# A hybrid trunk on one Trainium2 core: layer 0's scan outputs and output projections issued in pieces, with TensorE's order fixed by the program

## The chip, the cores and the metric

The kernel runs on one core of a Trainium2 chip. Its time is the device time of one run in microseconds (us); the number that counts is the median over runs. TensorE (PE) does the matrix products and the transposes, VectorE (DVE), ScalarE (ACT) and GpSimd (POOL) the elementwise work, and SyncE (SP) issues most transfers (DMAs).

## The reference

Two layers of a diffusion trunk over 1024 latent tokens and 128 context tokens, 1024 wide. Layer 0 runs window attention and a bidirectional state-space scan side by side and joins them in one output projection. The change lies in the last third of layer 0: the per-chunk output of the scan, its gated norm, the projection, and the gated residual with the norm that layer 1 starts with.

```python
def ssd_scan(x, dt, a_head, bm, cm, h0):          # once forward, once on flipped tokens
    ...                                            # chunks of 128 tokens; ch, bh: C and B of each head's group
    cum = jnp.cumsum(la, axis=2)
    diff = cum[:, :, :, None, :] - cum[:, :, None, :, :]
    decay = jnp.exp(jnp.where(causal, diff, -jnp.inf))
    scores = jnp.einsum("bclhn,bcshn->bclsh", ch, bh) * decay
    y_diag = jnp.einsum("bclsh,bcshp->bclhp", scores, xd)
    ...                                            # h_in: the state that enters each chunk
    y_off = jnp.einsum("bclhn,bchpn,bclh->bclhp", ch, h_in, jnp.exp(cum))
    y = (y_diag + y_off).reshape(b, L, H, P)

# y = y_forward + flip(y_backward) + d_skip * xs

def ab_output(attn, g, y, z, gnorm_w, w_out):
    a_out = attn.reshape(b, L, A_WIDTH) * jax.nn.silu(g)
    s_out = rms_norm(y.reshape(b, L, SSD_INNER) * jax.nn.silu(z), gnorm_w)
    return jnp.concatenate([a_out, s_out], axis=-1) @ w_out

# then xl = xl + gate * out, and layer 1: rms_norm(xl, norm_w[1]) * (1 + scale) + shift
```

There are 16 heads of 64 columns in two groups, so y of a chunk is 128 tokens by 1024.

## The kernel before, in words

Tokens are cut into nine tiles of 128: eight latent ones (0 to 7, NLT = 8) and the context tile, number 8. A tile is one chunk of the scan. Everything is fp32; a projection is done in three matmuls per weight tile, with each operand split into a high part and a rest (`split`, L244 to L253: the high part by ACT, the rest by a DVE subtraction, L250).

Who sets the order: the kernel is written tile by tile, and a scheduler with a model of the durations then puts the instructions of every engine into an order of its own; only data, buffers and a few marked instructions bind it. An engine runs what it is given strictly in that order. Transfers are issued by SP, likewise in an order, so one that waits for its buffer holds those behind it.

`scan_out` (L965) makes one chunk's scan output:
- It loads B and C (BC), forms both groups' C·B products on PE (Gp, L973), which ACT copies to SBUF (G), and loads xs, the silu of z (zs) and the states (H). POOL starts y with d_skip·xs (L985).
- For each group, and each direction, PE forms a 128x512 product with the state (off, L992), DVE scales it by the decays (L994) and POOL adds it to y (L995).
- For each group and each half of its heads (four heads), a buffer of cumulated decays (cu, two buffers for all) is loaded (L1000). POOL masks it, once per direction (L1003), ACT takes eight exponentials (L1005), DVE adds the two directions and multiplies by G (L1007, L1008), and PE does four small matmuls into yacc (L1011). So a chunk has four yacc groups, and each cu buffer comes free when its yacc group has been done. DVE adds yacc to y and multiplies by zs (L1012, L1013).
- The norm: ACT squares and sums y (L1015), POOL forms the root (`rstd_of`, L391, L392), DVE scales y (L1017), PE transposes y in two halves of four (pt, L1022), and each half is split into sT.

`project_out` (L1078) projects a tile: for each half of the 1024 output columns 12 weight tiles by three matmuls, 36 of 128x512 into acc (L256 to L258), then `residual` (L1056): DVE multiplies by the gate, POOL adds to x (L1061). ACT squares x, POOL forms the root, DVE scales it into xn (L1096), and `norm_T` (L1043) transposes xn in two halves on PE (pt, L1049), applies scale and shift on DVE (L1052, L1053, one buffer, nf) and stores each half as h1 (L1054). `project_operands` (L1070) loads and splits the attention half of the operands (raw, at).

PSUM: each tag has two buffers of 128x512 (L246): "pre" for Gp and off, "o" for yacc, "tr" for every pt, "mm" for acc.

The loop goes over context tile, tiles 0 to 7 and the end; in each step the program writes the scan output of tile c and then the projection of the tile before it. The scan outputs of the context tile and of tile 0 have been made already, beside the gates (`first_outputs`). During the last projection the loop drops its buffers and starts loading layer 1's weights.

## Time and profile before

| | |
|---|---|
| median of 3 runs | 1850.03 us (1843.2 to 1850.26) |
| the profiled execution | 1849.66 us, its span 1847.8 us |
| granted TensorE clock, mean | 0.958 of full speed |
| stage of the change (about 672 to 1000 us) | PE 292.1 us busy of 328, clock 0.92; DVE 230.9; ACT 149.3; POOL 175.3 |
| ahead of it, 672 us | PE 619.1 us busy, clock 0.97 |
| behind it, 848 us | PE 802.7 us busy, clock 0.96 |

The profile shows one execution. A row of a group of instructions reads: line, engine, operation, what it writes <- what it reads, partitions x elements, count | busy us, mean ns of one | idle us of the engine just before them, and what ended most of it. A row of the timeline reads: start us, length us, engine, line, operation, tiles, shape, count, and in brackets a wait ahead of it with what released it. A row of a stretch reads: its bounds, its length, busy us (and count) of PE, PE's weight loads, DVE, ACT, POOL, then the granted clock, the share of the transfers and GB/s. A row of waits reads: who waits <- for whom: us in all, number of waits, the longest. A row of the chain reads: start, us, engine, what. The names arenaF, arenaG, arenaR, arenaS are memory areas; tiles lie in them.

### The profile page before, as it was taken

Reading aid. Unit: us, or ns where it says so; the run is one execution under the profiler, and the core shown is the slowest. Engines: PE = TensorE matmul, PEld = TensorE weight load, DVE = VectorE, ACT = ScalarE, POOL = GpSimd, SP = SyncE. Lnnn points to the kernel's source line nnn. Section 1 sums busy time; section 2 is a strip of 40 time slices with the busy share of each in tenths; the row PEclk is TensorE's granted clock in tenths of the full one; section 3 lists DMA queues with packets and bytes.
Section 4 is the critical chain, followed back from the end, with each engine's and each line's share of the span. In section 5 each row is a group of like instructions: output and inputs, shape, how many; then the busy total and the mean of one; then the engine's idle time right before and its main releaser. Section 6 shows DMA issues by size and latency. Waiting matters only on the chain.

```text
span 1847.8 us, 27078 instructions
## 1 busy us (share of the span) xinstructions
PE 1713.8 (93%) x9031; PEld 1315.1 (71%) x9031; DVE 1045.4 (57%) x1989; ACT 817.2 (44%) x1873; POOL 744.2 (40%) x741
## 2 busy tenths in 40 slices
PE   6899999999998878998899999999999998998898
PEld 3799999877775766666688898655665665654486
DVE  4665545655546467777665434655665664564243
ACT  4532323665655354444444322444545544545321
POOL 3510000133343345665623010466666665565432
PEclk9999999999999888999999999899999998999899
DMA  7423423434435697565463532020120121104342
GB/s 260 125 81 93 121 62 111 131 101 132 115 105 146 195 284 240 166 208 159 167 180 85 165 110 79 11 61 23 52 71 23 45 75 28 37 29 122 109 154 91
DMA packets 210655, 210.26 MB, mean 114 GB/s; under 512 B 36162, under 2 KB 175504, under 8 KB 210516
## 3 DMA queue, kind: packets, MB, share of 16 engines
q1 hardware_dynamic: 210372, 208.40, 37.8%
q8 instruction: 72, 1.18, 0.3%
q14 instruction: 67, 0.55, 0.1%
q0 software_dynamic: 144, 0.13, 0.0%
HBM read 151.94 MB, written 51.72 MB: 110 GB/s over the span
## 4 chain that ended last, share of the span: by engine, by line
PE 65%; DMA 11%; DVE 8%; POOL 4%; ACT 3%; issue 3%; SPq 2%; POOLq 0%; DVEq 0%; ACTq 0%
PE acc L256 12%; PE acc L258 12%; PE acc L257 12%; PE acco L1469 6%; PE sc L1448 3%; PE pp L1427 3%; PE sc L1450 3%; PE sc L1449 3%; DMA arenaG<-cum_d 2%; DVE arenaR L250 2%; DMA arenaF<-rd_d 2%; DMA rd_d<-arenaF 2%; PE st L808 1%; DVE arenaF L209 1%; POOL arenaG L1003 1%
## 5 line engine op out<-in xcount | busy, mean ns | idle before, releaser
L256 PE MATMUL acc<-arenaR 128*128 128x384 f32 (+4 forms) x1248 | 426.7, 343 | 20.0 <-ACT arenaR L249 8.0
L1484 POOL TENSOR_TENSOR arenaG<-arenaG 128x512 f32<-128x512 f32 x256 | 332.6, 1318 | 233.8 <-ACT arenaG L1455 201.1
L257 PE MATMUL acc<-arenaR 128*128 128x384 f32 (+3 forms) x1176 | 398.2, 339 | 0.1
L258 PE MATMUL acc<-arenaR 128*128 128x384 f32 (+4 forms) x1152 | 385.9, 336 | 0.2
L256 PEld LDWEIGHTS acc<-arenaR 128*128 128x128 f32 x1248 | 240.0, 193 | 61.7 <-issue 16.0
L1455 ACT ACTIVATE arenaG<-sc 128x512 f32<-128x512 f32 (+1 forms) x304 | 174.7, 580 | 224.2 <-PE sc L1450 206.7
L209 DVE TENSOR_REDUCE arenaF<-pp 128x1 f32<-128x384 f32 (+1 forms) x400 | 198.8, 539 | 102.2 <-PE pp L1427 100.2
L257 PEld LDWEIGHTS acc<-arenaR 128*128 128x128 f32 x1176 | 226.4, 193 | 15.7 <-issue 3.6
L258 PEld LDWEIGHTS acc<-arenaR 128*128 128x128 f32 x1152 | 221.6, 192 | 16.5 <-DVE arenaR L250 2.3
L250 DVE TENSOR_TENSOR arenaR<-arenaF,arenaR 128x512 fp32r<-128x512 f32 (+2 forms) x144 | 133.2, 938 | 73.3 <-ACT arenaR L249 68.5
L249 ACT CAST arenaR<-arenaF 128x512 fp32r<-128x512 f32 (+3 forms) x160 | 101.0, 649 | 138.9 <-issue 22.6
L1469 PE MATMUL acco<-arenaG 128*64 128x512 f32 (+1 forms) x608 | 152.0, 612 | 0.0
L1005 ACT ACTIVATE arenaG<-arenaG,arenaF 128x128 f32<-128x128 f32 x288 | 88.4, 389 | 113.0 <-POOL arenaG L1003 112.7
L1427 PE MATMUL pp<-arenaR 96*128 96x384 f32 (+1 forms) x300 | 97.6, 387 | 12.8 <-DVE arenaF L209 12.5
L749 POOL TENSOR_TENSOR arenaG<-arenaF,arenaG 128x512 fp32r<-128x512 f32 x28 | 47.8, 1708 | 150.8 <-PE acco L753 87.0
L1448 PE MATMUL sc<-arenaR 96*128 96x512 f32 (+1 forms) x228 | 94.9, 416 | 5.6 <-ACT arenaG L1455 5.4
L1427 PEld LDWEIGHTS pp<-arenaR 96*128 96x128 f32 x300 | 58.6, 203 | 57.3 <-DVE arenaF L209 28.4
L1450 PE MATMUL sc<-arenaR 97*128 97x512 f32 (+1 forms) x228 | 90.6, 400 | 1.0 <-DMA arenaR<-arenaF 1.0
L258 PE MATMUL acc<-arenaR,arenaS 128*128 128x512 f32 (+1 forms) x240 | 90.6, 382 | 0.0
L1449 PE MATMUL sc<-arenaR 96*128 96x512 f32 (+1 forms) x228 | 89.9, 394 | 0.0
L1469 PEld LDWEIGHTS acco<-arenaG 128*64 128x64 f32 x608 | 37.3, 141 | 71.4 <-issue 68.3
L1003 POOL TENSOR_SCALAR_AFFINE_SELECT arenaG<-arenaG 128x512 f32<-128x512 f32 x72 | 60.2, 859 | 63.3 <-DMA arenaG<-cum_d 56.4
(328 smaller groups left out, 3331.9 us busy)
## 6 DMA issues: line engine op xcount, KB each, us to landing
arenaF<-in_ada_w_dram SPq DMA_DIRECT2D x96, 256.0 KB
arenaG<-cum_d SPq DMA_DIRECT2D x36, 512.0 KB
arenaF<-in_ab_w_in_dram SPq DMA_DIRECT2D x51, 256.0 KB
z_d<-arenaF SPq DMA_DIRECT2D x36, 128.0 KB
xs_d<-arenaF SPq DMA_DIRECT2D x8, 576.0 KB
arenaF<-xs_d SPq DMA_DIRECT2D x9, 512.0 KB
arenaF<-z_d SPq DMA_DIRECT2D x9, 512.0 KB
x_d<-arenaG SPq DMA_DIRECT2D x9, 512.0 KB
```

Of the source, the lines that this page charges most:

```text
L209: f()
L250: lo_eng.tensor_tensor(lo, src, hi.bitcast(F32), ALU.subtract)
L256: pe.matmul(out, ah, bh, start=first, stop=False)
L257: pe.matmul(out, ah, bl, start=False, stop=False)
L258: pe.matmul(out, al, bh, start=False, stop=last)
L1427: pe.matmul(pp[:, 0:w], AQ[s][0:96, t * 128:(t + 1) * 128], AK[s][0:96, k0:k0 + w], start=True, stop=True)
L1448: pe.matmul(sc[:, 0:n], AK[s][0:96, ks], BQ[s][:, qs], start=True, stop=False)
L1449: pe.matmul(sc[:, 0:n], BK[s][:, ks], AQ[s][0:96, qs], start=False, stop=False)
L1450: pe.matmul(sc[:, 0:n], AK[s][:, ks], AQ[s][:, qs], start=False, stop=True)
L1455: act.activation(pf, sc[:, 0:n], AF.Exp, scale=SCALE_M)
L1469: put = lambda: pe.matmul(acc[0][a * 64:(a + 1) * 64], V[:, a], pfs[a], start=(i < 2 and k < 2), stop=(last and k >= len(todo) - 2))
L1484: pool.tensor_tensor(totals[a], first[a] if i == 1 else totals[a], pfs[a], ALU.add)
```

## The change

- `TensorQueue` wraps PE: while `ordered` is set, each matmul and transpose is marked so that the scheduler must keep them in the order in which the program writes them. It is set for the loop and cleared behind it. The other engines and the transfers are ordered by the scheduler as before. All matmuls now bear the wrapper's line (L226) and all transposes L229; lines of `scan_out` move by 17 to 21 (L994 is L1011, L1007 and L1008 are L1025 and L1026, L1017 is L1038), those of `project_out` by 26 or 27 (L1096 is L1123), and L250 is L266, L391 and L392 are L407 and L408.
- `scan_out` becomes a generator of seven pieces: Gp with the first group's off products; the first yacc group; the second; the second group's off products; the third yacc group; the fourth; and the norm with the transposes of y.
- `project_out` becomes a generator of eight pieces: each half is cut behind its third, sixth and ninth weight tile and at its end, and the last piece forms xn. The transposes of xn (`norm_T`) are put on a list.
- The loop, for tile c: the first piece of c's scan, then what is left of the scan of c-1 (the norm and the transposes of y), then the postponed norm_T of tile c-2; then the projection of tile c-1, and behind its pieces 0, 2, 3, 4 and 5 one further piece of c's scan. The attention operands of tile c are fetched behind piece 2. The projection of the context tile runs with no scan beside it.

```diff
--- before.py
+++ after.py
@@ -213,6 +213,22 @@
             self.tick()
 
 
+class TensorQueue:
+
+
+    def __init__(self, tc, engine):
+        self.tc, self.engine, self.ordered = tc, engine, False
+
+    def put(self, ins):
+        return self.tc.keep_in_program_order(ins) if self.ordered else ins
+
+    def matmul(self, *a, **k):
+        return self.put(self.engine.matmul(*a, **k))
+
+    def transpose(self, *a, **k):
+        return self.put(self.engine.transpose(*a, **k))
+
+
 def bcast_rows(ap, n):
     return ap.unsqueeze(0).broadcast_to([n] + list(ap.shape))
 
@@ -220,7 +236,7 @@
 @with_exitstack
 def hybrid_trunk(ctx: ExitStack, tc: tile.TileContext, I, O, dbg=None, stage=99):
     nc = tc.nc
-    pe, act, dve, pool, dma = nc.tensor, nc.scalar, nc.vector, nc.gpsimd, nc.sync
+    pe, act, dve, pool, dma = TensorQueue(tc, nc.tensor), nc.scalar, nc.vector, nc.gpsimd, nc.sync
 
     cp = ctx.enter_context(tc.tile_pool(name="const", bufs=1))
     ps = ctx.enter_context(tc.tile_pool(name="ps", bufs=2, space=PSUM))
@@ -963,6 +979,7 @@
     sTs = {}
 
     def scan_out(p, sp, c):
+
         tok = slice(c * 128, (c + 1) * 128)
         BC = p.tile([128, 2, 2, 128], F32, tag="BC", name="BC", bufs=2)
         for d in range(2):
@@ -993,6 +1010,7 @@
                     t = p.tile([128, 512], F32, tag="rt", name="off", bufs=2)
                     dve.tensor_tensor(heads(t), heads(off), ex[:, d, c * 16 + g * 8:c * 16 + g * 8 + 8].unsqueeze(2).broadcast_to([128, 8, 64]), ALU.mult)
                     pool.tensor_tensor(y[:, cs], y[:, cs], t, ALU.add)
+            yield
             acc = psum("o" if c < NLT else "pre", "yacc")
             for u in range(2):
                 h0 = c * 16 + g * 8 + u * 4
@@ -1009,19 +1027,22 @@
                 for j in range(4):
                     hc = (u * 4 + j) * 64
                     pe.matmul(acc[:, hc:hc + 64], m[:, j], xs[:, g * 512 + hc:g * 512 + hc + 64], start=(u == 0 and j == 0), stop=(u == 1 and j == 3))
+                if u == 0:
+                    yield
             dve.tensor_tensor(y[:, cs], acc, y[:, cs], ALU.add)
             dve.tensor_tensor(y[:, cs], y[:, cs], zs[:, cs], ALU.mult)
+            yield
         ssq = p.tile([128, 1], F32, tag="ssq", name="ssq", bufs=4)
         act.activation(zs, y, AF.Square, accum_out=ssq)
         r = rstd_of(p, ssq, D, 1)
         dve.tensor_scalar(y, y, r, None, ALU.mult)
-        sT = sp.tile([128, 2, KT, 128], F32R, tag="sT", name="sT", bufs=2)
+        sT = sTs[c] = sp.tile([128, 2, KT, 128], F32R, tag="sT", name="sT", bufs=2)
         for q in range(2):
             pt = psum("tr", "pt")
             for j in range(4):
                 pe.transpose(pt[:, j * 128:(j + 1) * 128], y[:, (q * 4 + j) * 128:(q * 4 + j + 1) * 128], ident)
             split(sT[:, 0, q * 4:q * 4 + 4], sT[:, 1, q * 4:q * 4 + 4], pt.rearrange("p (k n) -> p k n", k=4))
-        return sT
+        yield
 
     p5 = Space(mem)
     p5.reserve("xn", D, 1, "G")
@@ -1029,7 +1050,8 @@
 
     def first_outputs():
         for c in (NLT, 0):
-            sTs[c] = scan_out(p5, op5, c)
+            for _ in scan_out(p5, op5, c):
+                pass
             yield
     p5.reserve("ar", 512, 2, "G")
     for _ in range(2):
@@ -1065,7 +1087,7 @@
         dma.dma_start(g, bcast_rows(gate_d[l, cond], 128))
         return g
 
-    operands5 = {}
+    operands5, norms = {}, []
 
     def project_operands(p, sp, t):
         tok = slice(t * 128, (t + 1) * 128)
@@ -1075,9 +1097,10 @@
         split(at[:, 0], at[:, 1], raw)
         return at
 
-    def project_out(p, sp, t, sT, gate, beside=None):
+    def project_out(p, sp, t, gate, beside=None):
+
         tok = slice(t * 128, (t + 1) * 128)
-        at = operands5.pop(t) if t in operands5 else project_operands(p, sp, t)
+        at, sT = operands5.pop(t), sTs.pop(t)
         x = p.tile([128, D], F32, tag="x", name="x", bufs=2)
         dma.dma_start(x, I["x_sample"][0, tok] if t < NLT else I["x_prompt"][0])
         for q in range(2):
@@ -1085,16 +1108,21 @@
             for k in range(12):
                 h, l = (at[:, 0, k], at[:, 1, k]) if k < 4 else (sT[:, 0, k - 4], sT[:, 1, k - 4])
                 mm3(acc, h, l, *wos[k, q], k == 0, k == 11)
+                if k in (2, 5, 8):
+                    yield
             residual(p, q, acc, x, gate)
-            if q == 0 and beside:
-                beside()
+            if q == 0:
+                if beside:
+                    beside()
+                yield
         dma.dma_start(x1_d[tok], x)
         ssq = p.tile([128, 1], F32, tag="ssq", name="ssq", bufs=4)
         xn = p.tile([128, D], F32, tag="xn", name="xn", bufs=1)
         act.activation(xn, x, AF.Square, accum_out=ssq)
         r = rstd_of(p, ssq, D, 1)
         dve.tensor_scalar(xn, x, r, None, ALU.mult)
-        norm_T(p, 1, 0 if t < NLT else 1, xn, tok)
+        norms.append(partial(norm_T, p, 1, 0 if t < NLT else 1, xn, tok))
+        yield
 
     w1 = I["mla_w_in"][0]
     wms = [Space(mem) for _ in range(4)]
@@ -1134,18 +1162,33 @@
     wp.drop("wr")
     with p5 as p:
         gate = load_gate(p, 0, 1)
-        prev = None
-        for c in [NLT] + list(range(NLT)) + [None]:
-            if c is not None:
-                sT = sTs[c] if c in sTs else scan_out(p, op5, c)
-            if prev is not None:
-                if c is None:
-                    p.drop("xs", "zs", "Hc", "cu", "y", "BC", "G")
-                    lp.close()
-                project_out(p, op5, prev[0], prev[1], gate, start_latents if c is None else None)
-                if prev[0] == NLT:
-                    gate = load_gate(p, 0, 0)
-            prev = (c, sT)
+        pe.ordered = True
+        running = None
+        for c in [0] + list(range(1, NLT)) + [None]:
+            prev = c - 1 if c else NLT if c == 0 else NLT - 1
+            scan = scan_out(p, op5, c) if c else iter(())
+            if c is None:
+                p.drop("Hc", "cu", "BC", "G")
+            next(scan, None)
+            if running:
+                for _ in running:
+                    pass
+            running = scan
+            if norms:
+                norms.pop()()
+            if c is None:
+                p.drop("xs", "zs", "y")
+                lp.close()
+            project = project_out(p, op5, prev, gate, start_latents if c is None else None)
+            for n, piece in enumerate(project):
+                if n in (0, 2, 3, 4, 5):
+                    next(scan, None)
+                if n == 2 and c is not None:
+                    operands5[c] = project_operands(p, op5, c)
+            if prev == NLT:
+                gate = load_gate(p, 0, 0)
+        norms.pop()()
+        pe.ordered = False
     if stage <= 5:
         dbg("X", x1_d, h1_d)
         return
```

The counts of instructions are the same on every engine. Three places show the order that each program is built to, at one tile in the middle of the loop.

On PE, around the start of a scan output, before (off, Gp and yacc belong to the scan of a tile, acc to a projection, the pt of L1022 are transposes of y, those of L1049 of xn):

```order
L992 MATMUL off<-arenaG,arenaF 128x512
L973 MATMUL Gp<-arenaF 128x128 x2
L1011 MATMUL yacc<-arenaF,arenaG 128x64 x4
L1022 MATMUL pt<-ident,arenaG 128x128 x8
L992 MATMUL off<-arenaG,arenaF 128x512 x2
L256 MATMUL acc<-arenaR,arenaS 128x512
L257 MATMUL acc<-arenaR,arenaS 128x512
L256 MATMUL acc<-arenaR,arenaS 128x512
L257 MATMUL acc<-arenaR,arenaS 128x512
L1011 MATMUL yacc<-arenaF,arenaG 128x64 x4
L1049 MATMUL pt<-ident,arenaG 128x128 x4
L258 MATMUL acc<-arenaR,arenaS 128x512
```

On PE, from the last yacc group of one tile to the third of the next, now (the first pt row is y of the tile before, the second xn of the one before that):

```order
L226 MATMUL yacc<-arenaF,arenaG 128x64 x4
L226 MATMUL acc<-arenaR,arenaS 128x512 x18
L226 MATMUL Gp<-arenaF 128x128 x2
L226 MATMUL off<-arenaG,arenaF 128x512 x2
L229 MATMUL pt<-ident,arenaF 128x128 x8
L229 MATMUL pt<-ident,arenaG 128x128 x8
L226 MATMUL acc<-arenaR 128x512 x9
L226 MATMUL yacc<-arenaF,arenaG 128x64 x4
L226 MATMUL acc<-arenaR 128x512 x3
L226 MATMUL acc<-arenaR,arenaS 128x512 x15
L226 MATMUL yacc<-arenaF,arenaG 128x64 x4
```

Small scan products, transposes and projection matmuls stood mixed singly; now both off products and all sixteen transposes stand in a row, with 18 projection matmuls ahead of them, and the yacc groups have 9 or 18 projection matmuls between them.

On DVE, at the scaling of y, before (L994 scales an off product and frees its PSUM buffer, L1007 and L1008 prepare a yacc group, L1017 scales y, L1096 forms xn, L250 is the rest of a split):

```order
L994 TENSOR_TENSOR arenaG<-off,arenaF 128x512 x2
L1007 TENSOR_TENSOR arenaG<-arenaG 128x4x128
L1008 TENSOR_TENSOR arenaG<-arenaG,arenaF 128x4x128
L1017 TENSOR_SCALAR arenaF<-arenaF 128x1024
L994 TENSOR_TENSOR arenaG<-off,arenaF 128x512
L1007 TENSOR_TENSOR arenaG<-arenaG 128x4x128
L1096 TENSOR_SCALAR arenaG<-arenaG,arenaF 128x1024
L250 TENSOR_TENSOR arenaR<-arenaG,arenaR 128x512
L1008 TENSOR_TENSOR arenaG<-arenaG,arenaF 128x4x128
L250 TENSOR_TENSOR arenaS<-pt,arenaS 128x512 x2
```

On DVE at the same place, now (L1011 was L994, L1025 and L1026 were L1007 and L1008, L1038 was L1017, L1123 was L1096, L266 was L250; L1082 multiplies by the gate):

```order
L1025 TENSOR_TENSOR arenaG<-arenaG 128x4x128
L1082 TENSOR_TENSOR arenaG<-acc,arenaF 128x512
L1038 TENSOR_SCALAR arenaF<-arenaF 128x1024
L1011 TENSOR_TENSOR arenaG<-off,arenaF 128x512
L1025 TENSOR_TENSOR arenaG<-arenaG 128x4x128
L1026 TENSOR_TENSOR arenaG<-arenaG,arenaF 128x4x128 x2
L1011 TENSOR_TENSOR arenaG<-off,arenaF 128x512
L266 TENSOR_TENSOR arenaS<-pt,arenaS 128x512
L1123 TENSOR_SCALAR arenaG<-arenaG,arenaF 128x1024
L266 TENSOR_TENSOR arenaS<-pt,arenaS 128x512
L1074 TENSOR_TENSOR arenaF<-pt,scl 128x512
```

The first off product's scaling (L1011) stood ahead of the scaling of y and now stands right behind it (L1038), and the scaling of x (L1123) comes after both scalings of off and the preparations of two yacc groups.

On POOL, ahead of the root that scales y, before (L1003 masks a decay buffer, L995 adds an off product to y, L1061 is a residual add, L391 and L392 form a root):

```order
L995 TENSOR_TENSOR arenaF<-arenaF,arenaG 128x512
L1003 AFFINE_SELECT arenaG<-arenaG 128x4x128 x2
L1061 TENSOR_TENSOR arenaG<-arenaG 128x512
L995 TENSOR_TENSOR arenaF<-arenaF,arenaG 128x512
L1003 AFFINE_SELECT arenaG<-arenaG 128x4x128 x2
L995 TENSOR_TENSOR arenaF<-arenaF,arenaG 128x512
L391 TENSOR_SCALAR arenaF<-arenaF 128x1 x2
L392 TENSOR_TENSOR arenaF<-arenaF,minus_half 128x1 x2
```

On POOL, now (L1021 masks, L407 and L408 form a root, L1083 is the residual add, L1012 adds an off product, L1002 starts the next y):

```order
L1021 AFFINE_SELECT arenaG<-arenaG 128x4x128 x4
L407 TENSOR_SCALAR arenaF<-arenaF 128x1
L408 TENSOR_TENSOR arenaF<-arenaF,minus_half 128x1
L1083 TENSOR_TENSOR arenaG<-arenaG 128x512
L1012 TENSOR_TENSOR arenaF<-arenaF,arenaG 128x512
L407 TENSOR_SCALAR arenaF<-arenaF 128x1
L408 TENSOR_TENSOR arenaF<-arenaF,minus_half 128x1
L1002 TENSOR_TENSOR arenaG<-arenaF 128x1024
```

The two roots stood together; now the root for y stands behind four masks in a row, ahead of the residual add, and the root for x behind the first add of an off product.

## The prediction

> **What bounds the kernel now.** I read the busy table first, then the stretch in which scan outputs and projections alternate, then who TensorE (PE) waits for there, then the chain.
>
> ```profile
> PE 1713.8 (93%) x9031; PEld 1315.1 (71%) x9031; DVE 1045.4 (57%) x1989; ACT 817.2 (44%) x1873; POOL 744.2 (40%) x741
> ```
> ```profile
> 765.44 0.75 DVE L1017 TENSOR_SCALAR arenaF<-arenaF 128x1024 f32<-128x1024 f32 x1 [2.94 <-POOL arenaF L392]
> ...
> 920.32 0.75 DVE L1017 TENSOR_SCALAR arenaG<-arenaG,arenaF 128x1024 f32<-128x1024 f32 x1 [2.94 <-POOL arenaF L392]
> ```
> ```profile
> 765.44:920.32 154.88, 137.29 (x656) 104.09 (x656) 112.45 (x135) 68.11 (x198) 96.70 (x96) 0.94 0.54 173
> ```
> ```profile
> PE yacc L1011 <- DVE arenaG L1008: 11.6, 5, 2.9
> PE pt L1022 <- DVE arenaF L1017: 3.2, 3, 1.2
> PE pt L1022 <- DVE arenaG L1017: 2.5, 2, 1.3
> ```
>
> L1017 scales a finished scan tile once per tile. Between the first row and the last lie five tiles, so a tile takes 154.88 / 5 = 31.0 us. The stretch's row gives PE 137.29 us busy at a granted clock of 0.94, DVE 112.45, POOL 96.70: PE is the fullest engine, but it idles 17.6 us of 154.88, 3.5 us a tile, and the wait rows say for whom: 11.6 + 3.2 + 2.5 us, all for DVE. So a tile is set by a chain, not by PE alone:
>
> ```profile
> 813.68 0.85 PE yacc L1011 x8
> ...
> 814.65 3.66 DMA arenaG<-cum_d
> ...
> 818.45 0.63 POOL arenaG L1003
> ...
> 819.11 1.06 ACT arenaG L1005 x4
> ...
> 821.56 0.69 ACT arenaF L1015
> ...
> 826.03 0.19 POOL arenaF L391
> ...
> 826.57 0.56 POOL arenaF L392
> ...
> 829.11 1.68 DVE arenaG L1096
> ```
>
> The reader sees one buffer of decay factors (cu) go round: a yacc group ends at 814.53, its buffer is reloaded, POOL masks it 3.9 us after the group's end (818.45), ACT's exponentials last until 821.56, and POOL's root of the tile's norm (L391, L392) follows.
>
> **What PE has to do for a tile** is unchanged. At full clock:
>
> ```profile
> 819.27 0.40 PE L257 MATMUL acc<-arenaR 128*128 128x512 f32 x1
> ...
> 824.05 0.39 PE L257 MATMUL acc<-arenaR 128*128 128x512 f32 x1
> ```
> ```profile
> 816.95 1.00 PE L1011 MATMUL yacc<-arenaF,arenaG 128*128 128x64 f32 x8
> 824.60 0.71 PE L973 MATMUL Gp<-arenaF 64*128 64x128 f32 x4
> 829.47 2.08 PE L992 MATMUL off<-arenaG,arenaF 64*128 64x512 f32 x4
> 835.12 0.60 PE L1049 MATMUL pt<-ident,arenaG 128*128 128x128 f32 x4
> ```
> ```profile
> 766.25 1.09 PE L1022 MATMUL pt<-ident,arenaF 128*128 128x128 f32 x8 [1.03 <-DVE arenaF L1017]
> ```
>
> 21 steps from 819.27 to 824.05 are 0.228 us each, so 72 projection matmuls 16.4 us; four yacc groups (eight records each) 4.0; four off products 4.1 (four records are two products); Gp 0.5 (the row overlaps its neighbour); eight y transposes 1.1; eight xn transposes 1.0. Sum 27.1 us. A fixed order can save at most 31.0 - 27.1 = 3.9 us a tile, 27 us over the seven.
>
> **The change, part by part.** The wrapper, the generators and the list of postponed norms issue the same instructions: nothing. The order on PE is the change, and it makes two places where PE meets a slower engine. I take the end of chunk c-1's last yacc group as zero. Behind it PE has 18 projection matmuls (4.1), Gp (0.5) and the first off product (1.0), and stands before the second off product at 5.6 us. That product needs a PSUM buffer: Gp and the off products share two, and in the built order it waits for DVE's L1011 on the first. On DVE L1011 now stands behind L1038, the scaling of y; L1038 waits for POOL's root, and POOL has that behind both masks of the buffer that the yacc group at zero has just set free. The durations, as means of the tiles in the loop:
>
> ```profile
> L1008 DVE TENSOR_TENSOR arenaG<-arenaG,arenaF 128x512 f32<-128x512 f32 x26 | 25.1, 967 | 0.7
> L1007 DVE TENSOR_TENSOR arenaG<-arenaG 128x512 f32<-128x512 f32 x26 | 22.6, 868 | 1.9 <-ACT arenaG L1005 1.0 <-issue 0.8
> L994 DVE TENSOR_TENSOR arenaG<-off,arenaF 128x512 f32<-128x512 f32 x24 | 16.4, 683 | 8.3 <-POOL arenaG L1061 8.3
> L250 DVE TENSOR_TENSOR arenaR<-arenaG,arenaR 128x512 fp32r<-128x512 f32 x5 | 11.9, 2385 | 0.0
> L1096 DVE TENSOR_SCALAR arenaG<-arenaG,arenaF 128x1024 f32<-128x1024 f32 x6 | 10.6, 1761 | 0.0
> L250 DVE TENSOR_TENSOR arenaS<-pt,arenaS 128x512 fp32r<-128x512 f32 x12 | 7.6, 675 | 0.0
> ```
> ```profile
> L1003 POOL TENSOR_SCALAR_AFFINE_SELECT arenaG<-arenaG 128x512 f32<-128x512 f32 x50 | 43.9, 900 | 43.4 <-DMA arenaG<-cum_d 40.9 <-PE acc L256 2.3
> L392 POOL TENSOR_TENSOR arenaF<-arenaF,minus_half 128x1 f32<-128x1 f32 x12 | 8.2, 702 | 0.5
> L985 POOL TENSOR_TENSOR arenaF<-arenaF 128x1024 f32<-128x1024 f32 x3 | 7.0, 2348 | 0.0
> ```
> ```profile
> 734.58 1.75 DVE L1017 TENSOR_SCALAR arenaG<-arenaG,arenaF 128x1024 f32<-128x1024 f32 x1 [0.45 <-POOL arenaF L392]
> ...
> 736.85 0.68 DVE L250 TENSOR_TENSOR arenaR<-arenaG,arenaR 128x512 fp32r<-128x512 f32 x1
> 737.46 0.74 DVE L1096 TENSOR_SCALAR arenaG<-arenaG,arenaF 128x1024 f32<-128x1024 f32 x1
> ```
>
> - First wait: reload 3.9, two masks 1.8, root 0.2 + 0.7, L1038, L1011 0.7, hand-overs 0.2. L1038 is 0.75 us (L1017 at 765.44) or 1.75 (at 734.58); I take 1.75, because POOL goes straight on to a residual add, as it goes on beside L1096 (1.76). Sum 9.25, so PE waits 9.25 - 5.6 = 3.65. Low end: 0.75 for L1038 and 0.63 for a mask (818.45): 2.1. High end: the reload sits in SP's queue behind the load of attention operands, which waits for a DVE subtraction of 2.385 us instead of 0.675: 1.7 more, 5.35.
> - Second wait: PE then does the second off product and the y transposes (1.0 + 1.1) and comes to the xn transposes, which before had a run of projection matmuls ahead of them. DVE has, behind L1011: L1025 (0.87), twice L1026 (0.97), L1011 (0.68), L266 (0.68), L1123 (1.76) = 5.9 us. DVE's neighbours overlap (736.85 and 737.46 start 0.61 apart, at 0.68 each), so 5.5, and PE waits 3.4. Low end, nothing held up: five of 0.6 and one of 0.7 (L1096 at 737.46) make 3.7, a wait of 1.6. High end, 5.9 with no overlap: 3.8.
> - Third: the xn transposes are stored in two halves through one buffer, and SP issues the next cu reload only behind both stores:
>
> ```profile
> 837.13 0.69 DVE L1053 TENSOR_TENSOR arenaF<-arenaF,shift 128x512 f32<-128x512 f32 x1
> ...
> 837.84 4.34 SPq L1054 DMA_DIRECT2D h_d<-arenaF  x2
> ...
> 840.37 0.69 DVE L1052 TENSOR_TENSOR arenaF<-pt,scl 128x512 f32<-128x512 f32 x1 [1.23 <-DMA h_d<-arenaF]
> ```
>
> From the first half's transposes: 1.4 on DVE, 2.5 until the store frees the buffer (837.84 to 840.37), 1.4, reload to mask 3.9, mask and exponentials 3.1 (818.45 to 821.56), L1025, L1082 and L1026 2.5, hand-overs 0.4: 15.2. PE has until the third yacc group 0.5 of transposes, 45 projection matmuls (10.2), two yacc groups (2.0), two off products (2.1): 14.8. Wait 0.4, between 0 and 2.
>
> - Moved with the steps: the attention operands' load, cast and subtraction stand a tile earlier in the program. Their cost is nothing while the next projection is a tile away; only SP's queue feels them (the 1.7 above). The gate is loaded once as before. The late drop of xs, zs, y only frees space.
> - The ends of the loop: before runs up to 24 projection matmuls (5.5 us) ahead at the first tile, and the last tile lacks the first wait. I take 0, bounds -6 and +6.
>
> Sum: 27.1 + 3.65 + 3.4 + 0.4 = 34.55 us a tile against 31.0, 3.55 more; times seven tiles, 24.9 us. The profiled execution took 1849.66 us, 0.4 under the median of 1850.03. Forecast 1849.7 + 24.9 + 0 = 1875 us. With all low ends (27.1 + 2.1 + 1.6 + 0) a tile takes 30.8 and the kernel 1848; with the high ends (38.25) 1900.
>
> **The Trainium skill against this sum.** The row that bears on it: after a wait of 3.06 us PE ran at about half rate.
>
> ```profile
> 655.49 3.68 PE L1011 MATMUL yacc<-arenaF,arenaG 128*128 128x64 f32 x16 [3.06 <-DMA arenaF<-xs_d]
> ...
> 660.68 0.52 PE L258 MATMUL acc<-arenaR 128*128 128x384 f32 x1
> 661.25 0.33 PE L257 MATMUL acc<-arenaR 128*128 128x384 f32 x1
> ```
>
> "TensorE: Matmul & The Clock Gate" (Part 1: The HAM clock gate) in the Trainium skill says that the array falls to half clock after about 3.4 us of idleness and needs as much sustained work to come back. By that rule waits of 3.65 and 3.4 us would sit on the edge; in this trace 3.06 already did it, so the trace is harsher than the rule. By the rule the sum is that of the first rival; without it, the forecast.
>
> "SBUF — State Buffer" (Who interferes with whom) in the Trainium skill says that VectorE and GpSimd lock a shared pair of SBUF ports for whole instructions, tensor_scalar among those that take it. The trace agrees: 0.75 and 1.75 us for the same L1017.
>
> **Rivals.**
> - The clock falls in every tile. After 655.49 sixteen yacc records took 3.68 instead of 2.0, and from 659.17 to 661.25 matmuls took 0.52 instead of 0.33, which loses 0.8 more: 2.5 in all. Added to each of seven tiles: 1875 + 17 = 1892. For it: two long waits close together, and transposes and small products between them. Against it: the waits of the loop so far, up to 2.9 us (the first wait row), leave the clock at 0.94.
> - The other side, not slower: DVE and POOL meet less in the new order, so that L1038 and L1123 take 0.75 and the adds 0.68. Then the two waits are 2.1 and 1.6 and the kernel stands at 1848; with the -6 of the ends, 1842. It turns where the waits together come to 3.9 us. For it: L1017 took 0.75 at both ends of the loop. Against: a residual add stands beside L1038 in the new order and L985's 2.35 us beside L1123, and L1096, which had L985 or an add beside it, took 1.76 as the mean of six.
> - PE does not wait because the order is hidden anyway: excluded, since the order on PE is fixed and its waits stand in the program.
>
> **How the numbers follow.** A measurement of this kernel tells about 0.5% (9 us) from no change. Forecast (1859 to 1888): 0.44. Clock falls, or SP's queue late too (1888 to 1906): 0.22; beyond that 0.05. Low ends, 1841 to 1859: 0.16; below, where a wait is missed by more than its low end or the ends of the loop gain more than 6 us: 0.13. Slower 0.71, same 0.16, faster 0.13. The range runs from 1842, all low ends with the -6 of the ends, to 1906, all high ends with their +6: it holds 0.44 + 0.22 + 0.16, about 0.8. The likeliest case's own range is 1859 to 1888.
>
> **What would show it.** Right: PE's wait rows name DVE's L1011 for off at 2 to 5 us and L1123 for pt at 2 to 4 us, seven times each, the waits for L1026 before yacc nearly gone, and y scalings 34 to 35 us apart. Wrong: off and pt waits together under 4 us a tile; L1038 at 0.75 us; or a lower granted clock than 0.94 there, which makes the clock rival right.

## The result, and the profile after

The changed kernel takes 1907.9 us (median of 4 runs, 1899.9 to 1909.8) against 1850.1 of the kernel before: 1.029 times as long, 95% interval 1.026 to 1.032. It is slower, as forecast, but by 57.8 us where 24.9 were forecast, and 2 us beyond the range. Of the runs below only one had executions far from the rest: two of nine of the lagged program with TensorE left to the scheduler took 3071 and 3222 us, and its time leaves them out.

The stretch of five full tiles after, from one scaling of y (L1038, L1017 before) to the fifth after it, and the waits of TensorE in the loop:

```profile
766.66 1.75 DVE L1038 TENSOR_SCALAR arenaF<-arenaF 128x1024 f32<-128x1024 f32 x1 [2.36 <-POOL arenaF L408]
...
959.98 1.75 DVE L1038 TENSOR_SCALAR arenaG<-arenaG,arenaF 128x1024 f32<-128x1024 f32 x1 [0.20 <-POOL arenaF L408]
```
```profile
766.66:959.98 193.32, 153.51 (x660) 114.50 (x660) 114.76 (x136) 69.87 (x202) 91.86 (x96) 0.83 0.45 140
```
```profile
PE off L226 <- DVE arenaG L1011: 20.2, 6, 4.2
PE pt L229 <- DVE arenaG L1123: 20.1, 7, 4.2
PE yacc L226 <- issue: 12.1, 8, 1.9
```

A tile takes 193.32 / 5 = 38.7 us against 31.0. The two waits that were read from the built order are there, under the names forecast: off for L1011, 3.4 us each (six times), and the transposes of xn for L1123, 2.9 us each (seven times). But the granted clock is 0.83 where it was 0.94. One tile on TensorE:

```profile
802.79 1.02 PE L226 MATMUL off<-arenaG,arenaF 64*128 64x512 f32 x2
808.04 2.07 PE L226 MATMUL off<-arenaG,arenaF 64*128 64x512 f32 x2 [4.23 <-DVE arenaG L1011]
810.05 1.97 PE L229 MATMUL pt<-ident,arenaG 128*128 128x128 f32 x8
814.69 1.94 PE L229 MATMUL pt<-ident,arenaG 128*128 128x128 f32 x8 [2.68 <-DVE arenaG L1123]
816.28 4.10 PE L226 MATMUL acc<-arenaR 128*128 128x512 f32 x9
...
836.61 1.38 PE L226 MATMUL yacc<-arenaF,arenaG 128*128 128x64 f32 x8 [1.92 <-issue]
837.75 5.71 PE L226 MATMUL acc<-arenaR,arenaS 128*128 128x512 f32 x18
```

The first off product takes 1.02 us, the same product behind the wait 2.07; eight transposes 1.97 instead of 1.0; nine projection matmuls 4.10 instead of 2.3. The stretches of 2 us say why (the column behind the five engines is the granted clock):

```profile
804.00:806.00 2.00, 0.00 (x0) 0.00 (x0) 0.36 (x1) 1.85 (x7) 1.83 (x5) 1.00 0.69 256
806.00:808.00 2.00, 0.00 (x0) 0.00 (x0) 2.00 (x3) 1.97 (x6) 0.84 (x1) 0.63 0.18 70
...
818.00:820.00 2.00, 2.00 (x6) 1.52 (x6) 0.33 (x1) 0.00 (x0) 0.00 (x0) 0.50 0.45 131
820.00:822.00 2.00, 2.00 (x14) 1.81 (x13) 1.05 (x2) 0.00 (x0) 0.00 (x0) 0.96 0.00 0
```

The clock halves inside the first wait and comes back only at about 820, twelve microseconds after work resumed: the second wait falls into the low stretch and prolongs it (the last section shows how). The chain behind the first wait, on POOL and DVE:

```profile
798.24 0.69 DVE L1032 TENSOR_TENSOR arenaG<-yacc,arenaG 128x512 f32<-128x512 f32 x1 [0.68 <-PE yacc L226]
...
803.47 1.23 POOL L1021 TENSOR_SCALAR_AFFINE_SELECT arenaG<-arenaG 128x512 f32<-128x512 f32 x2 [4.59 <-DMA arenaG<-cum_d]
...
805.06 0.55 POOL L408 TENSOR_TENSOR arenaF<-arenaF,minus_half 128x1 f32<-128x1 f32 x1
...
805.64 1.75 DVE L1038 TENSOR_SCALAR arenaG<-arenaG,arenaF 128x1024 f32<-128x1024 f32 x1 [2.60 <-POOL arenaF L408]
...
807.31 0.68 DVE L1011 TENSOR_TENSOR arenaG<-off,arenaF 128x512 f32<-128x512 f32 x1
```

The last yacc group ends at about 797.9; reload, masks, root, L1038 and L1011 follow, and L1011 ends 10.1 us later (9.25 forecast). L1038 takes 1.75 us, the value chosen.

The wait without a releaser ("issue") stands ahead of the fourth yacc group: DVE's L1026 ends at 836.50, and yacc starts at 836.61. Ahead of it DVE had waited for POOL's residual add, and L1025 and L1026 then took 1.16 and 1.63 us, against 0.69 and 0.93 a few microseconds before (829.16 and 830.37):

```profile
833.07 0.69 DVE L1011 TENSOR_TENSOR arenaG<-off,arenaF 128x512 f32<-128x512 f32 x1 [1.18 <-POOL arenaG L1083]
833.68 1.16 DVE L1025 TENSOR_TENSOR arenaG<-arenaG 128x512 f32<-128x512 f32 x1
834.87 1.63 DVE L1026 TENSOR_TENSOR arenaG<-arenaG,arenaF 128x512 f32<-128x512 f32 x1
```

### The profile page after: what moved, and what is told of

It reads as the page before. It is cut to its first block, busy times and chain, and to the rows that moved or that the text cites. A ratio compares the mean times of both kernels' runs of the same rounds, so it can differ in the third digit from the quotient of the medians.

```text
span 1905.3 us, 27105 instructions
## 1 busy us (share of the span) xinstructions
PE 1734.0 (91%) x9031; PEld 1332.3 (70%) x9031; DVE 1041.5 (55%) x1989; ACT 819.2 (43%) x1873; POOL 736.1 (39%) x741
## 4 chain that ended last, share of the span: by engine, by line
PE 39%; DMA 10%; DVE 5%; issue 3%; ACT 2%; SPq 1%; POOL 1%; POOLq 0%; DVEq 0%; ACTq 0%
PE acc L226 19%; PE sc L226 8%; PE acco L226 5%; DMA arenaG<-cum_d 3%; PE pp L226 3%; DMA rd_d<-arenaF 2%; DMA arenaF<-rd_d 2%; PE pt L229 2%; PE den L226 1%; PE yacc L226 1%; DVE arenaF L209 1%; DMA arenaF<-in_mla_w_in_dram 1%; DVE arenaR L266 1%; DVE arenaF L1315 1%; PE off L226 1%
## 5 line engine op out<-in xcount | busy, mean ns | idle before, releaser
L226 PE MATMUL acc<-arenaR 128*128 128x384 f32 (+4 forms) x3576 | 715.4, 344 | 20.7 <-ACT arenaR L265 9.8
L226 PEld LDWEIGHTS acc<-arenaR 128*128 128x128 f32 x3576 | 602.7, 196 | 94.9 <-issue 26.6
L226 PE MATMUL acco<-arenaG 128*64 128x512 f32 (+2 forms) x794 | 209.1, 562 | 9.0 <-POOL arenaG L765 7.4
L226 PE MATMUL sc<-arenaR 96*128 96x512 f32 (+3 forms) x684 | 200.9, 403 | 5.8 <-ACT arenaG L1498 4.4
L266 DVE TENSOR_TENSOR arenaR<-arenaF,arenaR 128x512 fp32r<-128x512 f32 (+2 forms) x144 | 129.4, 911 | 73.3 <-ACT arenaR L265 66.1
L265 ACT CAST arenaR<-arenaF 128x512 fp32r<-128x512 f32 (+3 forms) x160 | 101.0, 649 | 141.0 <-PE acc L226 38.7
L226 PEld LDWEIGHTS sc<-arenaR 96*128 96x128 f32 (+1 forms) x684 | 122.5, 192 | 50.7 <-ACT arenaG L1498 20.0
L226 PE MATMUL acc<-arenaR,arenaS 128*128 128x512 f32 (+2 forms) x576 | 155.9, 391 | 0.7 <-ACT arenaF L1246 0.7
L226 PEld LDWEIGHTS acco<-arenaG 128*64 128x64 f32 (+1 forms) x794 | 60.6, 139 | 92.3 <-issue 69.9
L226 PEld LDWEIGHTS acc<-arenaR,arenaS 128*128 128x128 f32 x576 | 110.0, 194 | 19.0 <-ACT arenaF L1246 1.0
L226 PE MATMUL pp<-arenaR 96*128 96x384 f32 (+1 forms) x300 | 97.3, 387 | 14.6 <-DVE arenaF L209 14.3
L1021 POOL TENSOR_SCALAR_AFFINE_SELECT arenaG<-arenaG 128x512 f32<-128x512 f32 x72 | 49.7, 714 | 144.9 <-DMA arenaG<-cum_d 121.7
L226 PEld LDWEIGHTS pp<-arenaR 96*128 96x128 f32 x300 | 58.2, 202 | 59.4 <-DVE arenaF L209 30.9
L226 PE MATMUL acc<-arenaS,arenaR 128*128 128x256 f32 (+1 forms) x560 | 90.7, 297 | 0.9 <-DVE arenaR L266 0.9
L266 DVE TENSOR_TENSOR arenaR<-acc,arenaR 64x512 fp32r<-64x512 f32 (+2 forms) x84 | 48.3, 579 | 61.6 <-ACT arenaR L265 60.1
L226 PEld LDWEIGHTS acc<-arenaS,arenaR 128*128 128x128 f32 x560 | 76.6, 191 | 1.9 <-PE acc L226 1.1
```

Source lines behind the costliest of these rows:

```text
L226: return self.put(self.engine.matmul(*a, **k))
L265: act.copy(hi, src)
L266: lo_eng.tensor_tensor(lo, src, hi.bitcast(F32), ALU.subtract)
L1021: pool.affine_select(cu[:, :, d], cu[:, :, d], [[0, 4], [s, 128]], ALU.is_ge, NEG, base=0, channel_multiplier=-s)
```

## The experiments

**The fixed order or the dealing?** The changed program with TensorE left to the scheduler:

```diff
-        pe.ordered = True
+        pe.ordered = False
```

> The changed program with ordered never set: the scheduler orders TensorE too, over the same pieces. Theory 1 (the fixed order on TensorE costs the time: two waits a tile, and half clock behind them): the waits for L1011 and L1123 go, the granted clock between 760 and 920 us is 0.93 or more, and the time is within 1840 to 1865. Theory 2 (the dealing in pieces costs the time by what it does to the orders of DVE, POOL and SP, whoever orders TensorE): 1890 or more.

1856.0 us, 1.002 of before (0.9999 to 1.0038). Five tiles took 163.50 us, 32.7 each:

```profile
768.07:931.57 163.50, 150.57 (x662) 109.92 (x660) 106.40 (x136) 67.98 (x199) 88.91 (x95) 0.92 0.53 165
```

The waits for L1123 are gone, and off products wait only 1.6 us in all for L1011, as the first theory had it; its clock of 0.93 or more was not reached (0.91 from 760 to 920). A full tile takes 1.7 us more than before, but in all the dealing in pieces costs next to nothing; the loss is the fixed order's. Its own counterpart fixes TensorE's order in the loop of before (the wrapper, `pe.ordered = True` ahead of that loop, whole scan outputs and whole projections):

> The kernel before with only the fixed order on TensorE: its loop as it was, a whole scan output and then a whole projection. Theory 1 (a fixed order pays each chain that its order does not cover): the third and fourth yacc group wait for a reload, masks and exponentials, 8 us, the transposes of y 7 and those of xn 7, with half clock behind them 3: a tile takes about 52 us instead of 31, 1960 to 2050. Rival (it is the dealing that costs, a fixed order is harmless): 1845 to 1870.

2014.8 us, 1.090 of before (1.087 to 1.093). Every chain that the order does not cover is a wait:

```profile
PE yacc L226 <- DVE arenaG L1024: 45.1, 7, 7.2
PE pt L229 <- DVE arenaG L1033: 39.3, 4, 14.3
PE pt L229 <- DVE arenaF L1033: 34.9, 5, 8.6
PE pt L229 <- DVE arenaG L1112: 30.6, 6, 5.1
```

So the dealing saves about 107 us of what a fixed order costs, and 58 are left.

**What does the clock cost by itself?** Useless matmuls in the two waits (`fill(n)` issues n matmuls of the projection's size whose result is not used):

```diff
+                    if pe.ordered and g == 0 and d == 1:
+                        fill(16)
                     off = psum("pre", "off")
...
             if norms:
+                fill(10)
                 norms.pop()()
```

> The changed kernel with useless projection matmuls in its two waits of each tile: 16 between the first and the second off product, 10 between the transposes of y and those of xn; their results are not used. Theory 1 (the half clock after a wait is a cost of its own): the clock stays near 1.0, the second off product takes 1.0 instead of 2.07, the transposes 1.0 instead of 1.95, the piece behind them 2.05 instead of 3 to 4 us; of these some 3.5 us a tile reach the end, 7 tiles, so 1908 falls to 1880 to 1890. Rival (the waits alone set the tile, what the clock loses lies in time that would be waited anyway): 1903 to 1912.

1889.1 us, 1.020 of before (1.016 to 1.023): 19 us less, by doing more. The stretch of five tiles and the same place in a tile:

```profile
769.91:945.95 176.04, 164.03 (x784) 123.83 (x783) 109.62 (x135) 69.21 (x202) 87.99 (x96) 0.98 0.48 154
```
```profile
809.45 1.12 PE L226 MATMUL off<-arenaG,arenaF 64*128 64x512 f32 x2
...
813.74 1.03 PE L229 MATMUL pt<-ident,arenaG 128*128 128x128 f32 x8
814.53 2.30 PE L226 MATMUL acc<-arenaR 128*128 128x512 f32 x9
```

A tile takes 35.2 us, 3.5 less, at a clock of 0.98. With the array kept busy the tile comes within 0.7 us of my sum of 34.55, in part by luck, since TensorE's own work is 26.0 us there and not the 27.1 of the sum (see below). The half clock is a cost of its own.

**Is the shared PSUM buffer the cause of the first wait?**

```diff
-        Gp = psum("pre", "Gp")
+        Gp = psum("o" if c < NLT else "pre", "Gp")
```

> The changed kernel with Gp in the PSUM tag of yacc, so that both off products find a buffer. Theory 1 (TensorE waits for a chain, yacc, masks, root, L1038, and the buffer is only its last link): the wait goes over to the transposes of y, for L1038, and is 1 to 2 us shorter a tile, as the second off product now lies in it: 1892 to 1901. Rival (the shared buffer is the cause): the 3.7 us go altogether with their half clock, 7 tiles: 1880 or less.

1913.5 us, 1.033 of before (1.029 to 1.037). The wait did go over to the transposes of y, but nothing was saved, so both theories missed the time: the wait for L1123 grew to 6.1 us a tile, 6.5 in the tile shown.

```profile
PE pt L229 <- DVE arenaG L1123: 42.9, 7, 7.3
```
```profile
809.98 4.05 DVE L1026 TENSOR_TENSOR arenaG<-arenaG,arenaF 128x512 f32<-128x512 f32 x2
...
814.16 0.55 POOL L408 TENSOR_TENSOR arenaF<-arenaF,minus_half 128x1 f32<-128x1 f32 x1
...
815.15 0.73 DVE L1123 TENSOR_SCALAR arenaG<-arenaG,arenaF 128x1024 f32<-128x1024 f32 x1
```

The root of xn now comes behind POOL's long adds (L1002 at 809.66 and L1012 at 811.78), and L1026 takes 2.0 us beside them, instead of 1.2 at this place in the changed kernel (2.35 for two).

**The second wait removed.** The transposes of xn behind the third piece (`if n == 2 and norms: norms.pop()()` in the loop over the pieces):

> The changed kernel with the transposes of xn put behind the third projection piece instead of ahead of the first. Theory 1: their wait of 2.7 us and the 1 us that they lose at half clock go, the first wait stays; 3.5 us times 7 tiles, 1880 to 1888. Rival (DVE is behind anyway, so that the next yacc group takes over the wait): 1900 or more, with waits for L1026 ahead of yacc.

1868.6 us, 1.009 of before (1.006 to 1.013): 39 us less, more than expected. Five tiles took 174.60 us, 34.9 each at a clock of 0.88, 3.8 less; over seven tiles that is 27, and the rest lies behind the full tiles. The wait ahead of the fourth yacc group grew from 1.5 to 2.4 us, which is the rival's mechanism at a small size. That one move takes back two thirds of the loss.

**Both transposes moved**, those of y behind the first piece (`if n == 0`, the rest of the scan before), those of xn behind the fourth, without and with Gp in the other tag:

> The fixed order with the transposes of y behind the first projection piece and those of xn behind the fourth. Theory 1: the y chain takes 9.3 us from the last yacc group, and TensorE has 4.1 + 0.5 + 2 + 2.05 us of work until then, so the y transposes wait about 1 us. In the built program the second off product now waits for the copy of Gp, which stands behind exponentials on ACT, 2 to 3 us. With one wait a tile of 2 to 3 us in place of 3.7 + 2.7 and its half clock: 1852 to 1865. Rival (DVE and POOL are what a tile takes now, so that other waits take over): 1866 or more, as with the xn transposes alone moved.

> As the run before, and Gp in the PSUM tag of yacc, so that the second off product has a free buffer. Theory 1: only the y transposes wait, about 1 to 2 us a tile, the clock stays near 1.0, a tile takes 28 to 29.5 us against 31.0 of the kernel before: 1835 to 1850. Rival (another wait takes over, as when Gp alone was moved): 1860 or more.

1871.0 us (1.012 of before, 1.010 to 1.014) and 1873.4 us (1.014, 1.011 to 1.016). Here the rival was right: moving more brought nothing over the move of xn alone. The waits of the two runs:

```profile
PE off L226 <- DVE arenaG L1011: 14.9, 3, 6.1
PE off L226 <- ACT arenaF L992: 13.0, 4, 4.6
```
```profile
PE yacc L226 <- issue: 20.1, 12, 3.1
PE pt L229 <- DVE arenaG L1038: 12.8, 4, 5.5
PE pt L229 <- DVE arenaF L1038: 6.2, 4, 2.2
```

In the first, the copy of Gp (L992, at 865.38) stands behind seven exponentials (from 863.32); in the second, L1038 is still late (866.03), because POOL still has two masks (863.87) ahead of the root (865.18). Cover counted from the old order did not hold in either.

**One tile of lag.** The projection of c-2 beside the scan of c, and, with the pieces counted from 0 as in the code, the transposes of y behind piece 2, those of xn behind piece 3, yacc four behind piece 6:

```diff
+        tiles = [NLT] + list(range(NLT))
+        for i, t in enumerate(tiles):
+            c = i + 1 if i + 1 < NLT else None
...
+                if n == 2:
+                    for _ in running or ():
+                        pass
+                    running = scan
+                if n == 3 and norms:
+                    norms.pop()()
+                if n in (0, 2, 3, 4, 6):
+                    next(scan, None)
```

> The fixed order, with the projection one tile further behind: beside the scan of tile c runs the projection of c-2, so that the norm of y(c-1) has a whole projection to hide behind; the transposes of y stand behind the third projection piece, those of xn behind the fourth, the last yacc group behind the seventh. Theory 1 (a fixed order costs what its order does not cover): no wait for L1038 or L1123 is left; the second off product may still wait 0 to 3 us for a PSUM buffer; a tile takes 27.5 to 30.5 us, the two projections at the end run without a scan beside them; 1825 to 1855. Rival (in a fixed order the other engines' orders, made by the scheduler, always open a new wait of 2 us or more with half clock behind it): 1860 to 1880.

> As the run before, with Gp in the PSUM tag of yacc. Theory 1: the wait of the second off product is gone as well, 0 to 3 us a tile less than the run before: 1825 to 1845. Rival: Gp or yacc wait instead, no gain over the run before, or a loss.

> The same lagged program with TensorE left to the scheduler. Theory 1: the scheduler finds its cover in either program, so this stays within 1840 to 1860 like the kernel before and the unordered dealing, and whatever the lagged order gains is the fixed order's. Rival (the lag itself gives the gain): as fast as the fixed order, within 3 us.

The lag alone took 1864.0 us (1.006 of before, 1.004 to 1.009), with Gp in the other tag 1849.9 (0.999, 0.997 to 1.001), and with TensorE left to the scheduler, Gp in its old tag, 1861.1 (1.005, 1.003 to 1.007). The first took the time of the rival, and freeing TensorE changed little in it, 2.9 us, as the last run's rival had it. The second gained 14 us over the first and missed its range of 1825 to 1845 by 5. The waits for L1123 are gone from it, and that for L1038 is down to 0.8 us in all; a new one stands out, for the PSUM buffers of the y transposes, which stand one piece ahead of those of xn:

```profile
PE pt L229 <- DVE arenaS L266: 14.0, 12, 2.4
```

Two runs space the two further apart (xn behind piece 5; y behind piece 1 and xn behind piece 4), and a third leaves TensorE to the scheduler in the latter:

> The lagged fixed order with Gp in the tag of yacc, and the transposes of xn two pieces later, behind the sixth projection piece, so that the PSUM buffers of the y transposes have been read by then. Theory 1 (each uncovered chain is one wait with its half clock): the two waits for L266, 14 us in the loop, go with the slow off products behind them (0.9 us a tile): 15 to 20 us less than the 1849.9 of the run with the transposes behind the fourth piece, 1828 to 1838. Rival (the scheduler's orders on DVE, ACT and POOL give the time back elsewhere): 1843 to 1855, with as much waiting ahead of yacc.

> The same with the transposes of y behind the second piece and those of xn behind the fifth: three pieces between them, but one piece less for the y chain, 9.5 us of cover for a chain of 9.3 to 11. Theory 1: a wait of 0 to 2 us for L1038 in place of the waits for L266: 1832 to 1845. Rival: 1843 to 1855 as in the run before.

> The lagged dealing with Gp in the tag of yacc, the transposes of y behind the second piece and those of xn behind the fifth, with TensorE left to the scheduler. Theory (a fixed order without gaps is what gains): 1852 to 1865, like the other unordered versions. Rival (the lag and the places of the transposes gain, whoever orders TensorE): within 4 us of 1843.

1843.9 us (0.997 of before, 0.995 to 0.999) and 1843.0 us (0.997, 0.995 to 0.999). Both beat both kernels, by 7 us over before. The time of the first is its rival's, the loss of those waits having brought 6 us instead of 15 to 20; that of the second lies in both its ranges, but its waits for L1038, 8.4 us in eight, have taken the place of those for L266, as its theory had it. Freed, the second took 1852.9 us (1.001, 1.000 to 1.003): this gain, small as it is, is the fixed order's. The full tiles of the two fixed ones, four and five of them:

```profile
784.98:898.96 113.98, 102.24 (x530) 77.48 (x528) 85.46 (x109) 55.34 (x160) 74.93 (x77) 1.00 0.59 190
```
```profile
778.76:913.39 134.63, 125.09 (x649) 96.15 (x647) 99.07 (x133) 64.72 (x184) 87.67 (x90) 1.00 0.59 189
```

28.5 and 26.9 us a tile at a clock of 1.00, against 31.0 before. Of that gain, 2.5 to 4.1 us a tile, 7 us in all reach the end. One place where it goes is the start. There the scan of tile 1 now runs beside the first projection, and yacc waits long, with half clock behind it; the same stretch of the run with xn behind piece 5, and of the kernel before:

```profile
700.00:720.00 20.00, 9.90 (x32) 7.48 (x33) 14.59 (x19) 8.54 (x22) 6.14 (x7) 0.50 0.73 246
```
```profile
712.03 1.94 PE L226 MATMUL yacc<-arenaF,arenaG 128*128 128x64 f32 x8 [6.88 <-ACT arenaG L1023]
```
```profile
700.00:720.00 20.00, 19.68 (x92) 15.55 (x92) 14.04 (x21) 7.69 (x20) 5.61 (x6) 0.95 0.69 217
```

TensorE works 9.9 of these 20 us instead of 19.7.

**The ends of the loop.** The order fixed up to tile 6 only, and the reverse (`c is None or c == NLT - 1` in the same place):

```diff
+            pe.ordered = c is not None and c < NLT - 1
             prev = c - 1 if c else NLT if c == 0 else NLT - 1
```

> The changed kernel with TensorE's order fixed up to tile 6 and left to the scheduler in the last two steps of the loop (tile 7's scan and the last projection). Theory (the fixed order at the end costs 15 to 23 us of its own): 1885 to 1893. Rival (the end costs what any tile costs, 7.7 us): 1898 to 1903.

> The reverse: the order fixed in the last two steps alone. Theory: 1856 of the unordered dealing and 15 to 23 more, 1871 to 1879. Rival: 1862 to 1866.

1891.8 us (1.022 of before, 1.019 to 1.025) and 1865.2 us (1.009, 1.005 to 1.012). The last two steps give back 16 us when they are freed, and cost 9 over the 1856.0 of the unordered dealing when they alone are fixed. The first agrees with a cost of their own, the second with that of an ordinary tile; the two losses over before, 39.5 and 12.9, nearly add up to the 57.8. So the fixed order costs 9 to 16 us in the last two steps, where an ordinary tile costs 7.7; why the two runs differ is open.

## Why the prediction was wrong, point by point

- **What bounds a tile: right.** A chain through POOL and DVE, not TensorE's work, set the waits; the places and the names of the two long ones came as read from the built order. The first of them came six times and not seven: at the first scan of the loop TensorE waits 0.74 us for the copy of Gp instead.
- **First wait, 3.65 forecast: right**, 3.7 measured in the five full tiles (3.1 to 4.2). L1038 took 1.75 us, as chosen. **Second wait, 3.4: right in kind**, 2.7 there. **Third, 0.4 ahead of the third yacc group: wrong place.** It was 1.6 us ahead of the fourth, where DVE waits for POOL's residual add, a step that the sum did not follow. So waits ahead of yacc are not nearly gone, as one of the signs had it: 12.1 us (the issue row), against 12.6 for L1008 before. Together the three are 8.0 us a tile against 7.45.
- **TensorE's work, 27.1: too high.** With the clock at 1.00 a tile keeps it busy for 102.24 / 4 = 25.6 us in the run with xn behind piece 5. In the filled run, whose order is that of the changed kernel, it is 26.0: 33.8 us from one first off product to the next (804.63 to 838.40), less 6.3 of fill and 1.5 of waiting. The off row of before, 2.08 us for four records, was itself at half clock (the row below, the kernel before); four records at full clock take 1.13.

```profile
830.00:831.60 1.60, 1.60 (x5) 0.12 (x1) 1.60 (x2) 0.17 (x1) 1.60 (x2) 0.50 0.59 218
```

- **The clock, 0 in the forecast: the step that failed.** The sum took all of TensorE's work as done at full clock. TensorE is busy for 153.51 / 5 = 30.7 us a tile, 4.7 to 5.1 more than the 26.0 or 25.6 at full clock; with the 8.0 of waits that makes up the 38.7 measured. This splits the measured time and tests nothing; the test is the filled run, where filling the waits brought back 3.5 us a tile. The first rival named this mechanism, for the reason that came true (two waits close together, and small work between them), but priced it at 2.5 us, from one wait with steady work behind it, and gave it 0.22. That loops with waits up to 2.9 us had kept 0.94 was taken as evidence against it; those waits had projection matmuls between them, and the 0.94 already held 3.4 us of half clock in each of the five tiles (the row above lies in one of these stretches). After the change it is 13.0 us a tile.
- **The rule on the clock gate in the Trainium skill ("TensorE: Matmul & The Clock Gate", Part 1: The HAM clock gate)**, idleness first and then sustained work until the clock returns, gave the right rival. The trace agrees on the shape, but its 3.4 us is here the step in which the clock changes (last section), not the idleness that it takes: from 803.8, where the first wait began, to 806.5, where the mean of 0.63 puts the fall, are 2.7 us, and a wait of 1.92 was enough elsewhere.
- **The ends of the loop, 0 with bounds of 6: open.** Of the 57.8 us five full tiles hold 5 x 7.7 = 38.5, and 19 lie outside, where the sum had 7.1 for two more tiles. The scalings of y place them: against before, the second starts 1 us earlier, the third 1 later, the eighth 40 and the ninth, the last, 52 later (994.85 against 942.45), and the kernel ends 57 later. Seven tiles at the measured price would leave 4 us for the ends, inside the bounds; the runs on the last two steps put these at 1.5 and 8 us more than a tile. The longest wait of the loop, 10.5 us for L1038 at its start (734.34), delays nothing by itself: that scaling starts at 733.52, and at 734.58 before.
- **The other-side rival** fell: L1038 took 1.75 us in every full tile.

## What to carry to other kernels

A fixed order on one engine is a promise about all others: go along it, and ask at each instruction what its operand's chain will have done by then. Each gap is a wait, and waits also cost clock. Here one wait of 1.92 us put 3.4 us of the work behind it at half clock, and waits of 3.7 and 2.7 us, with only an off product and eight transposes between them, kept TensorE there for 10 to 14 us. So price the half clock for every wait of about that length, and look in the trace before the change for the stretches that are already there. A whole tile of lag, with Gp in the other tag, did better here (1849.9 us) than transposes moved by a piece or two (1868.6 to 1873.4). The other engines are ordered anew each time, so count the cover again on the new program.

## What the runs showed of the hardware

The clock changed only at points 3.41 us apart. A row of 2 us at 0.63 was at full clock for 0.52 us of its length and at half clock for the rest, so the clock fell at 806.52; from the 0.96 of 820 to 822 it came back at 820.16. Three rows further on (here with the busy time of TensorE alone) show the next fall, at 837.24, and the return at 840.64:

```profile
836.00:838.00 2.00, 1.39 (x9) 0.81 0.03 10
838.00:840.00 2.00, 2.00 (x5) 0.50 0.80 221
840.00:842.00 2.00, 2.00 (x9) 0.84 0.86 250
```

The four points are 13.64, 17.08 and 3.40 us apart, 4, 5 and 1 times 3.41. Rows of 1 us, worked out in the same way, put all 23 changes of this run between 680 and 1000 us on such points, and the 17 of the kernel before too. In the five full tiles 19 steps are at half clock, 13.0 us a tile; before there were 5, 3.4 us a tile.

A step that TensorE spent in part idle did not bring the clock back here. The four steps from 806.52 held 1.9, 2.1, 2.1 and 3.4 us of work, and only the last ended the half clock; the step from 837.24 held 3.4 and ended it at once. So the second wait prolongs what the first began. Short waits decide narrowly: behind waits of 1.62 us the 18 projection matmuls took 4.37 us, behind 1.92 they took 5.71. The length alone does not decide, since in the kernel before a wait of 1.22 us, ahead of the transposes of y at 827.96, was followed by half clock from 828.4; what else does is open.

```profile
875.32 1.08 PE L226 MATMUL yacc<-arenaF,arenaG 128*128 128x64 f32 x8 [1.62 <-issue]
876.20 4.37 PE L226 MATMUL acc<-arenaR,arenaS 128*128 128x512 f32 x18
```
